# Cross-attention heads in three hi and lo passes instead of full fp32, with Strassen blocks moved between single chunks

## The chip, the cores and the metric

The kernel runs on one core of one Trainium2 chip. The metric is the device time of one execution in microseconds. The core has TensorE (PE; its weight loads are shown as PEld), VectorE (DVE), ScalarE (ACT), GpSimd (POOL) and SyncE (SP), which run side by side and wait for each other by semaphores. Transfers are issued from queues of SP, POOL and ACT.

## The reference

One decoder layer over 256 tokens of 1024 channels, all in float32. The part that the change touches is branch C, cross-attention of four heads of 128 channels into 256 memory tokens:

```python
def memory_cross_attention(q, mem_n, w_mem_kv):
    mk, mv = jnp.split(mem_n @ w_mem_kv, 2, axis=-1)
    # q, mk, mv are cut into XATTN_HEADS = 4 heads of 128
    lg = jnp.einsum('bshd,bmhd->bhsm', qh, kh).astype(jnp.float32) * (HEAD_DIM ** -0.5)
    p = jax.nn.softmax(lg, axis=-1).astype(q.dtype)
    return jnp.einsum('bhsm,bmhd->bshd', p, vh).reshape(B, S, C_WIDTH)

h = rms_norm(x, norm_g[layer])
(qa, ka, va, ga, ub, vb, gb, qc, gc, ma, mb, mc) = split_cols(h @ w_in[layer], IN_SPLITS)
out_c = memory_cross_attention(qc, rms_norm(mem, ...), w_mem_kv[layer]) * jax.nn.silu(gc)
y = sigmoid(ma) * (out_a @ w_branch_a) + sigmoid(mb) * (out_b @ w_branch_b) + sigmoid(mc) * (out_c @ w_branch_c)
return rms_norm(x + y @ w_out)
```

Branch A is causal attention with six heads of 128, branch B a gated product of tokens in chunks of 128.

## The kernel before, in words

**Chunks.** All weights pass TensorE in an order written out by `plan()`. A chunk is 128 x 1024 weights. For each chunk ScalarE makes a rounded high part (`split_hi`, L260, type fp32r) and VectorE the remainder (`split_lo`, L264); a product of two such numbers is then three fp32r passes, hi x hi, hi x lo and lo x hi (`mm3`, L448 to L450, and the same written out elsewhere). The kinds of chunk:

- "mvk" (8): memory values and keys; "tok" (4): part of the values of A and B; 
- "fea" (30): one head of q, k, qc, or 128 channels of a gate; `mm_fea`, L630, 8 passes of 512 columns and 8 of 256;
- "st" (70): the remaining input columns, by a Strassen scheme with seven products of half blocks; a block is two chunks of `mm_st`, L570, six passes of 512 columns each. Their weights are summed in two "form" buffers: loaded on SP (L233), added to by transfers on POOL (L236) or by VectorE (L240);
- "br" (16) and "out" (8): the branch and output projections, with `mm3`.

Chunks are split four ahead of their use, into five slots. Pairs of chunks that are not Strassen share one "raw" buffer; `load` (L214) fills it when the second chunk of the pair two before it is split.

**Planner.** Everything else is a list of units with an engine, an estimated duration, what it comes after, and a due chunk (class `Units`, L85 to L148). While the program is written out, `slot` puts a unit in ahead of or behind a chunk when its engine has room by the estimates, or when it is due. TensorE units must be ready by the estimate with 1.8 us to spare, or due. On the chip each engine then follows its own written order.

**Cross heads.** The queries are evicted by `join_half` (L633) to tile "cx"; the memory keys too, then multiplied by the memory's norm (`mkf`, L658); the values by `evict_mv` (L604, L608). Four chains for each head follow: `cs` with `c_scores` (L882, L886: two fp32 products of 256 columns), the maximum (L891) and the exponentials; `cn` normalizes; `cp` transposes (L781) and evicts the transposed weights (`c_pT_out`, L901); `cv` is `c_pv` (L903, L908: two fp32 products of 256 columns) and the eviction of the result (L914). Rope of branch A moves pairs of q and k by transfers on the SP queue (L769).

**Where order binds.** `cx` is one tile. Tiles of one tag share memory: a new tile waits for the last reader of the old one. "ga" and "gc" belong to the gates' chunks, "sg0" and "sg1" to the first gate's sums, "och" and "ocl" to the memory rows first and branch C's output later.

Of the kernel before, what the change touches and what calls it, by code (L numbers as in the profile page):

```python
# [24 lines left out]
F32 = mybir.dt.float32  # L25
# [3 lines left out]
OP = mybir.AluOpType  # L29
# [20 lines left out]


def plan():


    p = [("mvk", 0), ("vvb", 0)]
    st = [("st", (g, i)) for g in range(FAST) for i in ORDER]
    late = st[24:]
    del st[24:]
    for what in ("qc0", "", "qc2", "", "q0", "", "q1", "", "", "q2", "", "q3", "", "", "q4", "", "", "q5",
                 "", "", "ga0", "", "ga2", "", "", "ga4", "", "", "gc0", "", "", "gc2", "", "ub4", "", "", "gb4", "", ""):  # L60
        if not what:
            p.append(st.pop(0))
        elif what[0] == "q" and what[1] != "c":
            p += [("q", int(what[1])), ("k", int(what[1]))]
        else:
            p += [(what[:2], int(what[2]) + i) for i in range(2)]
    assert not st, len(st)
    br = [("br", ((h, a), (g, b))) for h, a, g, b in ((0, 0, 0, 1), (1, 0, 1, 1), (0, 2, 1, 2), (0, 3, 0, 4),
                                                      (0, 5, 1, 3), (1, 4, 1, 5), (0, 6, 0, 7), (1, 6, 1, 7))]
    for piece, n in zip(br, (2, 1, 2, 2, 2, 1, 1, 0)):  # L70
        p += [piece] + late[:n]
        del late[:n]
    return p
# [78 lines left out]
def tile_hybrid_layer(ctx: ExitStack, tc: tile.TileContext, mw, xT, mem, x, fin_g, ln_g, w, ws, w_sp, b_sp, b_spt, rope, out):  # L152
# [37 lines left out]
    for name, g in PLAN:  # L190
        if name == "mvk":
            chunks += [("mvk", HALVES[2 * i], HALVES[2 * i + 1]) for i in range(KD)]
        elif name in TOK:
            chunks += [("tok", name, g * 512, 2 * i) for i in range(4)]
        elif name in ("st", "br"):
            chunks += [("st", *g, i) if name == "st" else ("br", *g[i]) for i in range(2)]
# [7 lines left out]
    n_all = len(chunks)  # L204
    PLAIN = [j for j in range(n_all // 2) if chunks[2 * j][0] != "st"]

# [3 lines left out]
    def load_part(j, a, b):  # L210
        src = bass.AP(tensor=w.tensor, offset=w.offset + PLAIN.index(j) * 128 * PIECE + a, ap=[[PIECE, 128], [1, b - a]])
        nc.sync.dma_start(raw[j][:, a:b], src)

    def load(j):  # L214
        raw_alloc(j)
        parts = 2 if 18 <= j < 47 else 1
        for i in range(parts):
            load_part(j, i * PIECE // parts, (i + 1) * PIECE // parts)
# [31 lines left out]
    def split_alloc(c):  # L250
# [5 lines left out]
        hi[c], lo[c] = V["hi"][:, c % SPL, :], V["lo"][:, c % SPL, :]  # L256

    def split_hi(c, a=0, b=CH):
        o = (c % 2) * CH
        nc.scalar.activation(hi[c][:, a:b], raw[c // 2][:, o + a:o + b], AF.Copy)  # L260

    def split_lo(c, a=0, b=CH):
        o = (c % 2) * CH
        nc.vector.tensor_tensor(lo[c][:, a:b], raw[c // 2][:, o + a:o + b], hi[c][:, a:b].bitcast(F32),  # L264
                                OP.subtract)
# [353 lines left out]
    def mm_fea(c):  # L619
        _, name, h = chunks[c]  # L620
        src = V["n"]


        p = acc_bank()
        pa, pb = p[:, 0:S], p[:, S:2 * S]
        long = [(p, hi[c][:, hsl(k)], src[:, k].rearrange("p a s -> p (a s)")) for k in range(KD)]
        short = [(pa, lo[c][:, hsl(k)], src[:, k, 0, :]) for k in range(KD)]
        passes = short + long if c % 2 else long + short
        for i, (o, wt, m) in enumerate(passes):
            nc.tensor.matmul(o, wt, m, start=i == 0, stop=i == len(passes) - 1, skip_group_check=True)  # L630
        join_half(name, h, c, p)

    def join_half(name, h, c, p):  # L633
# [18 lines left out]
        elif name in ("qc", "mk"):  # L652
            i = int(name == "mk")
            cross_tile()
            join(V["cx"][:, i, h, :])
            if i and h % 2:
                u = V["cx"][:, 1, h - 1:h + 1, :]
                U.add(f"mkf{h}", DVE, 0.7, lambda: nc.vector.tensor_tensor(  # L658
                    u, u, bc["m"][:, None, :].to_broadcast([128, 2, S]), OP.mult),
                    after=[f"mk{h - 1}", f"mk{h}", "mrms"], first=True)  # L660
        elif name == "ub":
# [220 lines left out]
    def c_scores(h):  # L882
        cx = V["cx"]
        ST["cs", h] = ps = bank()
        for t in range(2):
            nc.tensor.matmul(ps[:, t * S:(t + 1) * S], cx[:, 0, h, tsl(t)], cx[:, 1, h, :], start=True, stop=True)  # L886

# [11 lines left out]
    def c_pT_out(h):  # L899
        ST["cT", h] = work.tile([128, 512], F32, name="pt", tag="pt", bufs=3)  # L900
        nc.scalar.activation(ST["cT", h], ST["cp", h], AF.Copy)  # L901

    def c_pv(h):  # L903
        p = ST["cT", h]
        mv = V["cx"][:, 2].rearrange("p (t a) b -> p t (a b)", t=2)
        ST["co", h] = ps = bank()
        for m in range(2):
            nc.tensor.matmul(ps[:, 0:S], mv[:, m, hsl(h)], p[:, m * S:(m + 1) * S], start=m == 0, stop=m == 1)  # L908

    def c_out(h):  # L910
# [3 lines left out]
        nc.scalar.activation(V["oc"][:, h, :], ST["co", h][:, 0:S], AF.Copy)  # L914

    for h in range(HC):
# [6 lines left out]
        U.chain(f"cp{h}", (PE, 0.44, lambda h=h: c_pT(h)), (ACT, 0.62, lambda h=h: c_pT_out(h)), after=[f"cn{h}"] + back("v", h))  # L923
        U.chain(f"cv{h}", (PE, 0.88, lambda h=h: c_pv(h)), (ACT, 0.4, lambda h=h: c_out(h)), after=[f"cp{h}", "mve"])

# [233 lines left out]
    for c in range(n_br + 4):  # L1159
# [14 lines left out]
        for e in {5: (), 6: (), 7: (9,), 8: (11,), 9: (12, 13)}.get(c, (s,) if s > 3 else ()):  # L1174
            if chunks[e][0] == "st":
                raw[e // 2] = form_tile(buf(*chunks[e][1:3]))
                came = ready[e]
            else:
                came = {4: 24.0, 5: 25.5}.get(e // 2, 0.0)
# [6 lines left out]
        s += c == 9  # L1186
        if s % 2 == 1 and s // 2 in PLAIN:
            q = PLAIN.index(s // 2) + 2
            if 4 < q < len(PLAIN):
                load(PLAIN[q])  # L1190
            if q == 6:
                load_mem()
# [132 lines left out]
```

## Time and profile before

| | |
|---|---|
| time, median of 3 runs | 316.98 us (316.41 to 317.22) |
| profiled execution | 316.41 us, span 314.7 us |
| TensorE | busy 307.0 us, 98% of the span |
| VectorE | 259.8 us, 83% |
| ScalarE | 228.2 us, 73% |
| GpSimd | 36.4 us, 12% |
| mean granted TensorE clock | 0.995 |

The span runs from the first to the last instruction. Busy time of TensorE counts overlapped passes once. A group's row has its line in the kernel, engine, operation, out<-in by the program's names, shapes, a count, and then busy us, mean ns of one, and idle time before it. A row of waits names who waited for whom, us in total, times, and the longest. A row of a timeline or of the chain has start and length in us.

### The profile page before, as it was taken

The page shows a single profiled execution, that of the slowest core. Times are in us where ns is not written, and L with a number is a line of the kernel's source. Part 1 is how long each engine was busy: PE and PEld are TensorE (multiplying, and loading weights), DVE is VectorE, ACT ScalarE, POOL GpSimd, SP SyncE. Part 2 cuts the span into 40 slices and gives each one's busy share as a digit, 9 for nine tenths or more (in the row PEclk, how much of TensorE's full clock was granted, in tenths as well). Part 3 has the DMA queues.
Part 4 walks back from the last instruction along what each step waited for, and adds up shares of the span by engine and source line. Part 5 has one row for each costly group of instructions (what it writes and reads, how often), then busy time and mean ns, then how long its engine had stood idle before and what let it go on. Part 6 is the DMA issues. An engine that isn't in the chain of part 4 may idle for free.

```text
span 314.7 us, 4438 instructions
## 1 busy us (share of the span) xinstructions
PE 307.0 (98%) x1542; PEld 259.1 (82%) x1542; DVE 259.8 (83%) x376; ACT 228.2 (73%) x357; POOL 36.4 (12%) x55
## 2 busy tenths in 40 slices
PE   7999999999999999999999999999999999999992
PEld 3888888888888888888888888888888887888982
DVE  2879998996689888877499799999896699989532
ACT  3876989556997668877996978778759565486333
POOL 1000040030011013005002102004010031000022
PEclk9999999999999999999999999999999999999997
DMA  7999999779659869958966999778999989943003
GB/s 194 408 390 421 403 351 234 305 209 202 190 187 237 293 214 223 209 204 187 323 202 175 192 336 292 166 246 189 219 347 274 313 212 194 394 147 133 2 5 129
DMA packets 20470, 75.14 MB, mean 239 GB/s; under 512 B 2656, under 2 KB 3680, under 8 KB 18016
## 3 DMA queue, kind: packets, MB, share of 16 engines
q1 hardware_dynamic: 15984, 59.00, 52.1%
q0 software_dynamic: 4320, 15.73, 27.6%
q8 instruction: 12, 0.20, 0.2%
q10 hardware_dynamic: 144, 0.13, 0.1%
q14 instruction: 10, 0.08, 0.1%
HBM read 73.02 MB, written 1.05 MB: 235 GB/s over the span
## 4 chain that ended last, share of the span: by engine, by line
PE 82%; DMA 7%; DVE 4%; issue 3%; ACT 2%; POOL 0%; ACTq 0%; SPq 0%; POOLq 0%; DVEq 0%
PE acc L630 27%; PE acc L570 18%; DMA form<-in_ws_dram 6%; PE aux L570 5%; PE acc L508 4%; PE acc L450 3%; PE acc L448 3%; PE acc L449 3%; PE aux L502 3%; DVE lo L264 2%; PE aux L781 2%; PE acc L481 2%; PE aux L481 2%; DMA raw<-in_w_dram 2%; PE aux L449 1%
## 5 line engine op out<-in xcount | busy, mean ns | idle before, releaser
L264 DVE TENSOR_TENSOR lo<-form,hi 128x1024 fp32r<-128x1024 f32 x70 | 84.8, 1221 | 15.4 <-ACT hi L260 14.8
L260 ACT ACTIVATE hi<-form 128x1024 fp32r<-128x1024 f32 x70 | 73.5, 1058 | 23.5 <-DMA form<-in_ws_dram 9.7
L264 DVE TENSOR_TENSOR lo<-raw,hi 128x1024 fp32r<-128x1024 f32 x58 | 70.1, 1222 | 10.2 <-ACT hi L260 10.0
L260 ACT ACTIVATE hi<-raw 128x1024 fp32r<-128x1024 f32 x58 | 60.9, 1057 | 9.0 <-DMA raw<-in_w_dram 2.7
L630 PE MATMUL acc<-n,hi 128*128 128x512 f32 x240 | 60.2, 393 | 0.0
L236 POOL DMA_DIRECT2D form<-in_ws_dram x30 | 26.1, 871 | 229.2 <-DVE lo L264 83.3
L630 PEld LDWEIGHTS acc<-n,hi 128*128 128x128 f32 x240 | 44.0, 188 | 8.5
L570 PE MATMUL acc<-hi,s 128*128 128x512 f32 x96 | 32.7, 398 | 0.0
L630 PE MATMUL acc<-n,lo 128*128 128x256 f32 x240 | 32.6, 285 | 0.0
L630 PEld LDWEIGHTS acc<-n,lo 128*128 128x128 f32 x240 | 31.3, 191 | 1.3
L570 PE MATMUL acc<-hi,n 128*128 128x512 f32 x72 | 24.8, 401 | 0.0
L570 PEld LDWEIGHTS acc<-hi,s 128*128 128x128 f32 x96 | 18.0, 188 | 3.7
L570 PE MATMUL aux<-hi,s 128*128 128x512 f32 x64 | 20.7, 389 | 0.0
L570 PE MATMUL acc<-lo,s 128*128 128x512 f32 x48 | 18.7, 389 | 0.0
L570 PE MATMUL aux<-hi,n 128*128 128x512 f32 x48 | 15.8, 391 | 0.0
L570 PEld LDWEIGHTS acc<-hi,n 128*128 128x128 f32 x72 | 13.5, 188 | 2.7
L570 PEld LDWEIGHTS aux<-hi,s 128*128 128x128 f32 x64 | 12.0, 188 | 2.5
L570 PE MATMUL acc<-lo,n 128*128 128x512 f32 x36 | 14.0, 390 | 0.0
L643 ACT ACTIVATE qk<-acc 128x256 f32<-128x256 f32 x12 | 4.7, 389 | 11.1 <-PE acc L630 11.0
L570 PE MATMUL aux<-lo,s 128*128 128x512 f32 x32 | 12.6, 393 | 0.1
L240 DVE TENSOR_TENSOR form<-form,form 128x1024 f32<-128x1024 f32 x10 | 12.2, 1220 | 0.0
L570 PEld LDWEIGHTS aux<-hi,n 128*128 128x128 f32 x48 | 9.0, 188 | 1.9
(233 smaller groups left out, 578.7 us busy)
## 6 DMA issues: line engine op xcount, KB each, us to landing
raw<-in_w_dram SPq DMA_DIRECT2D x18, 1024.0 KB, 8.4
form<-in_ws_dram SPq DMA_DIRECT2D x30, 512.0 KB, 6.0
form<-in_ws_dram POOLq DMA_DIRECT2D x30, 512.0 KB, 8.4
raw<-in_w_dram SPq DMA_DIRECT2D x22, 512.0 KB, 6.9
st<-in_mw_dram SPq DMA_DIRECT2D x7, 384.0 KB, 7.4
raw<-in_w_dram SPq DMA_DIRECT2D x8, 256.0 KB, 6.9
xk<-in_x_dram SPq DMA_DIRECT2D x2, 512.0 KB, 7.3
xt<-in_xT_dram SPq DMA_DIRECT2D x2, 512.0 KB, 8.4
```

Of the source, the lines that this page charges most:

```text
L236: nc.gpsimd.dma_start(form_half(i, h), block(g, b, h), accum_op=OP.add)
L240: nc.vector.tensor_tensor(form_half(i, h), form_half(i, h), form_half(1 - i, h), OP.add)
L260: nc.scalar.activation(hi[c][:, a:b], raw[c // 2][:, o + a:o + b], AF.Copy)
L264: nc.vector.tensor_tensor(lo[c][:, a:b], raw[c // 2][:, o + a:o + b], hi[c][:, a:b].bitcast(F32), OP.subtract)
L448: nc.tensor.matmul(p, s_hi, m_hi, start=first, stop=False)
L449: nc.tensor.matmul(p, s_hi, m_lo, start=False, stop=False)
L450: nc.tensor.matmul(p, s_lo, m_hi, start=False, stop=last)
L481: nc.tensor.matmul(acc[name, o][t], src[:, k0 + i, tsl(t)], wt[c][:, i * 512:(i + 1) * 512], start=c == 8 and i + j == 0, stop=c == 11 and ...
L502: nc.tensor.matmul(acc["mv", 0][t][:, a:b], src[:, k, tsl(t)], wt[:, a:b], start=k + n == 0, stop=k == KD - 1 and n == len(parts) - 1)
L508: nc.tensor.matmul(p, wt, m, start=k == 0 and j < HC, stop=k == KD - 1 and j >= HC)
L570: nc.tensor.matmul(p, x[:, k0 + k, tsl(t)], wt[c][:, a * 512:(a + 1) * 512], start=first and a + j == 0, stop=half == 1 and a + j == 3, sk ...
L630: nc.tensor.matmul(o, wt, m, start=i == 0, stop=i == len(passes) - 1, skip_group_check=True)
```

## The change

The cross heads' products go through `mm3`. For that the queries, the keys, the values and the transposed weights each get a high part (ScalarE) and a low part (VectorE), in tiles that lie in tags not in use at that time. `cp` and `cv` get due chunks, counted back from the first ga chunk. The order is written out chunk by chunk in a string, in which "." is one Strassen block; against the order before, one block now stands between q1 and k1 (before: behind k1), one between q2 and k2 (before: behind k2), one between ga0 and ga1 (before: behind ga1). The other chunks keep their order. Loads are numbered by pairs of plain chunks, with the same pairs and the same parts.

```diff
+SEQUENCE = ("qc0 qc1 . qc2 qc3 . q0 k0 . q1 . k1 . q2 . k2 q3 k3 . . q4 k4 . . q5 k5 . . ga0 . ga1 ga2 ga3 . . "
+            "ga4 ga5 . . gc0 gc1 . . gc2 gc3 . ub4 ub5 . . gb4 gb5 . . w00 w01 . . w10 w11 . w02 w12 . . w03 w04 "
+            ". . w05 w13 . . w14 w15 . w06 w07 . w16 w17")
...
-    for what in ("qc0", "", "qc2", "", "q0", "", "q1", "", "", "q2", "", "q3", "", "", "q4", "", "", "q5",
-                 "", "", "ga0", "", "ga2", "", "", "ga4", "", "", "gc0", "", "", "gc2", "", "ub4", "", "", "gb4", "", ""):
...
     def evict_mv():
-        cross_tile()
+        for n, tag in (("mvh", "gc"), ("mvl", "ga")):
+            slot_tile(n, [128, 2, CW], tag, F32R)
         for t in range(2):
-            h = V["cx"][:, 2, 2 * t:2 * t + 2, :].rearrange("p a b -> p (a b)")
-            nc.scalar.activation(h, acc["mv", 0][t], AF.Copy, scale=rstm[:, t:t + 1])
+            p, f = acc["mv", 0][t], rstm[:, t:t + 1]
+            h = V["mvh"][:, t, :]
+            nc.scalar.activation(h, p, AF.Copy, scale=f)
+            later(f"mvl{t}", DVE, 0.7, scaled_lo, V["mvl"][:, t, :], p, f, h, due=now[0] + 2)
...
+                def hi_part():
+                    if n + "h" not in V:
+                        slot_tile(n + "h", [128, HC, S], high, F32R)
+                        slot_tile(n + "l", [128, HC, S], low, F32R)
+                    nc.scalar.activation(V[n + "h"][:, hs, :], u, AF.Copy)
...
+                U.chain(f"{name}l{h}", (ACT, 0.62, hi_part),
+                        (DVE, 0.7, lambda: sub_lo(V[n + "l"][:, hs, :], u, V[n + "h"][:, hs, :])),
+                        after=[f"mkf{h}"] if i else [f"qc{h - 1}", f"qc{h}", "mrow"], first=True,
+                        due=10 ** 6 if i else c + 4)
...
         for t in range(2):
-            nc.tensor.matmul(ps[:, t * S:(t + 1) * S], cx[:, 0, h, tsl(t)], cx[:, 1, h, :], start=True, stop=True)
+            mm3(ps[:, t * S:(t + 1) * S], V["qch"][:, h, tsl(t)], V["qcl"][:, h, tsl(t)], V["mkh"][:, h, :],
+                V["mkl"][:, h, :], True, True)
...
-        ST["cT", h] = work.tile([128, 512], F32, name="pt", tag="pt", bufs=3)
+        ST["cT", h] = work.tile([128, 512], F32R, name="pt", tag="pt", bufs=3)
         nc.scalar.activation(ST["cT", h], ST["cp", h], AF.Copy)
 
+    def c_pT_lo(h):
+        if h < 2:
+            slot_tile(f"ptl{h}", [128, 512], ("ub", "v1")[h], F32R)
+        sub_lo(V[f"ptl{h % 2}"], ST["cp", h], ST["cT", h])
...
-            nc.tensor.matmul(ps[:, 0:S], mv[:, m, hsl(h)], p[:, m * S:(m + 1) * S], start=m == 0, stop=m == 1)
+            ms = slice(m * S, (m + 1) * S)
+            mm3(ps[:, 0:S], V["mvh"][:, m, hsl(h)], V["mvl"][:, m, hsl(h)], p[:, ms], low[:, ms], m == 0, m == 1)
...
-        U.chain(f"cs{h}", (PE, 0.88, lambda h=h: c_scores(h)), (DVE, 0.9, lambda h=h: c_max(h)),
+        U.chain(f"cs{h}", (PE, 0.72, lambda h=h: c_scores(h)), (DVE, 0.9, lambda h=h: c_max(h)),
...
-                after=[f"qc{h}", f"mkf{h | 1}", "sqrts"] + back("p", h))
+                after=[f"qcl{h | 1}", f"mkl{h | 1}", "sqrts"] + back("p", h))
...
+        U.chain(f"cp{h}", (PE, 0.44, lambda h=h: c_pT(h)), (ACT, 0.62, lambda h=h: c_pT_out(h)), after=[f"cn{h}"] + back("v", h), due=[G0 - 12 + h, G0 - 11 + h])
+        U.chain(f"cv{h}", (DVE, 0.68, lambda h=h: c_pT_lo(h)), (PE, 0.72, lambda h=h: c_pv(h)), (ACT, 0.4, lambda h=h: c_out(h)),
+                after=[f"cp{h}", "mvl0", "mvl1"], due=[G0 - 10 + h, G0 - 6 + h, G0 - 5 + h])
```

More of the change, by code (lines that the diff above doesn't have):

```diff
@@ L56, in plan @@
     st = [("st", (g, i)) for g in range(FAST) for i in ORDER]
-    late = st[24:]
-    del st[24:]
-    for what in ("qc0", "", "qc2", "", "q0", "", "q1", "", "", "q2", "", "q3", "", "", "q4", "", "", "q5",
-                 "", "", "ga0", "", "ga2", "", "", "ga4", "", "", "gc0", "", "", "gc2", "", "ub4", "", "", "gb4", "", ""):
-        if not what:
+    for what in SEQUENCE.split():
+        if what == ".":
             p.append(st.pop(0))
-        elif what[0] == "q" and what[1] != "c":
-            p += [("q", int(what[1])), ("k", int(what[1]))]
+        elif what[0] == "w":
+            p.append(("br", (int(what[1]), int(what[2]))))
         else:
-            p += [(what[:2], int(what[2]) + i) for i in range(2)]
+            p.append((what[:-1], int(what[-1])))
     assert not st, len(st)
[L68 to L72, printed above, removed]
     return p
@@ L194, in tile_hybrid_layer @@
             chunks += [("tok", name, g * 512, 2 * i) for i in range(4)]
-        elif name in ("st", "br"):
-            chunks += [("st", *g, i) if name == "st" else ("br", *g[i]) for i in range(2)]
+        elif name == "st":
+            chunks += [("st", *g, i) for i in range(2)]
+        elif name == "br":
+            chunks.append(("br", *g))
         else:
@@ L203, in tile_hybrid_layer @@
             chunks += [("out", c, kh * 4), ("out", c, kh * 4 + 2)]
-    n_all = len(chunks)
-    PLAIN = [j for j in range(n_all // 2) if chunks[2 * j][0] != "st"]
+    PLAIN = [c for c, k in enumerate(chunks) if k[0] != "st"]
+    place = {c: divmod(m, 2) for m, c in enumerate(PLAIN)}
     def raw_alloc(j):
@@ L215, in load @@
         raw_alloc(j)
[L216 removed]
+        parts = 2 if 12 <= j < 22 else 1
         for i in range(parts):
@@ L627, in mm_fea @@
         short = [(pa, lo[c][:, hsl(k)], src[:, k, 0, :]) for k in range(KD)]
-        passes = short + long if c % 2 else long + short
+        passes = short + long if place[c][1] else long + short
         for i, (o, wt, m) in enumerate(passes):
@@ L1186, in tile_hybrid_layer @@
         s += c == 9
[L1187 to L1190, printed above, removed]
+        if place.get(s, (0, 0))[1]:
+            q = place[s][0] + 2
+            if 4 < q < len(PLAIN) // 2:
+                load(q)
             if q == 6:
@@ L1254, in tok @@
         return m.reshape(2, 4, 128, 512).transpose(0, 2, 1, 3).reshape(-1)
-    def fea(ms):
-        r = np.stack([m.reshape(KD, 128, 128) for m in ms]).transpose(2, 0, 1, 3)
-        return r.reshape(-1)
     wkv = np.asarray(w_mem_kv)[0]
@@ L1272 @@
     for name, g in PLAN:
-        if name == "st":
-            continue
-        if name == "br":
-            parts.append(np.stack([br[i] for i in g], axis=1).reshape(-1))
+        if name in ("st", "br"):
+            if name == "br":
+                two.append(br[g].reshape(128, -1))
         elif name == "mvk":
@@ L1281 @@
         else:
-            two.append(cols[name][:, g * 128:(g + 1) * 128])
-            if len(two) == 2:
-                parts.append(fea(two))
-                two = []
+            two.append(cols[name][:, g * 128:(g + 1) * 128].reshape(KD, 128, 128).transpose(1, 0, 2).reshape(128, -1))
+        if len(two) == 2:
+            parts.append(np.stack(two, axis=1).reshape(-1))
+            two = []
     w = np.concatenate(parts + [wo.reshape(-1)])
```

35 lines of the change are left out of this document (19 added, 16 removed).

## The prediction

> **What bounds the kernel now.** I read the page first, then TensorE's waits, then the chain of work that ended last in order of time, then timelines of single stretches.
>
> ```profile
> span 314.7 us, 4438 instructions
> PE 307.0 (98%) x1542; PEld 259.1 (82%) x1542; DVE 259.8 (83%) x376; ACT 228.2 (73%) x357; POOL 36.4 (12%) x55
> ...
> PEclk9999999999999999999999999999999999999997
> ```
>
> TensorE is busy for 98% of the span at the full granted clock. Its own waits, in the whole run:
>
> ```profile
> PE aux L354 <- PEq L1314: 0.8, 1, 0.8
> PE acc L508 <- ACT hi L422: 0.8, 1, 0.8
> ```
>
> Both lie in the first 8 us. Between them and the output's last products TensorE is never seen idle, so the span is the sum of what TensorE streams, plus head and tail. Whatever takes TensorE time away shortens the span by that much, as long as the engines that feed it keep up.
>
> The cross heads' products stand in that chain. Columns are start, length in us, and the work; "x" counts records, two for each fp32 product of 256 columns:
>
> ```profile
> 67.27 2.59 PE aux L886 x12
> ...
> 94.18 1.73 PE aux L908 x8
> 95.91 0.86 PE aux L886 x4
> ...
> 101.37 0.86 PE aux L908 x4
> ...
> 112.41 0.86 PE aux L908 x4
> ```
>
> That is 2.59 + 1.73 + 0.86 + 0.86 + 0.86 = 6.90 us for 32 records, 0.216 us each, 0.43 us for a product.
>
> **The products.** Four heads have two score products and two value products each, 16 in all. Each becomes three fp32r passes of 256 columns: 48 passes. The timeline of TensorE shows passes of that form, each with its own weight load, in the fea chunks and (the same helper of three passes) at the end:
>
> ```profile
> 79.75 2.08 PE L630 MATMUL acc<-n,lo 128*128 128x256 f32 x16
> 81.66 2.00 PE L630 MATMUL acc<-n,hi 128*128 128x512 f32 x8
> ...
> 293.14 0.28 PE L448 MATMUL aux<-hi,y 128*128 128x256 f32 x1
> ...
> 293.85 0.40 PE L1105 MATMUL aux<-xks,identr 128*128 128x256 f32 x2
> ```
>
> From 79.75 to 81.66 there are 16 passes: 0.119 us each. From 293.14 to 293.85 there are 6: 0.118. I take 0.120, rounded up. New cost 48 x 0.12 = 5.76 us; saved 6.90 - 5.76 = **1.14 us**. The bounds are narrow: 0.118 gives 1.24, 0.125 would give 0.90.
>
> The Trainium skill, "FP8 and Floating Point Precision", section "TensorE Precision Notes", says that true FP32 takes four passes through the array. By that rule alone three passes leave 3/4 of 6.90, a saving of 1.73 us and a median of 315.25. The rows say less, because a reduced-precision pass of 256 columns takes 0.12 us and a quarter of an fp32 product only 0.108; the rows decide.
>
> **What is added on VectorE and ScalarE.** Prices by groups of like instructions (count, busy us, mean ns):
>
> ```profile
> L993 DVE TENSOR_TENSOR obl<-aux,obh 128x512 fp32r<-128x512 f32 x2 | 1.4, 684 | 0.0
> L970 DVE SCALAR_TENSOR_TENSOR ut<-aux,b_col,ut 128x256 f32<-128x256 f32 x4 | 1.7, 476 | 0.0
> L877 DVE SCALAR_TENSOR_TENSOR vb<-vb,lst,lng 128x768 f32<-128x768 f32 x2 | 2.0, 1012 | 0.0
> L729 ACT ACTIVATE n<-xt 128x512 fp32r<-128x512 f32 x4 | 2.5, 625 | 0.0
> ```
>
> - Splits of the queries and of the memory keys, two pairs each: ScalarE 4 x 0.63 = 2.5 us, VectorE 4 x 0.68 = 2.7 us.
> - Low part of the memory values: two scalar_tensor_tensor of 512 columns, halfway between 476 and 1012 ns, 0.74 each: 1.5 us. The high part replaces an eviction of the same size.
> - Low part of the transposed weights, one per head: 4 x 0.68 = 2.7 us on VectorE.
>
> VectorE gets 6.9 us and ScalarE 2.5 us more. None of it is on the path if it fits into their slack. Where it falls:
>
> ```profile
> 39.40:64.50 25.10, 25.10 (x135) 21.74 (x135) 24.18 (x33) 19.50 (x29) 3.59 (x8) 1.00 0.87 282
> 64.50:92.80 28.30, 28.30 (x154) 24.64 (x153) 21.39 (x30) 22.21 (x40) 3.45 (x4) 1.00 0.80 203
> 92.80:116.00 23.20, 23.20 (x118) 19.75 (x117) 21.42 (x40) 15.98 (x27) 1.81 (x3) 1.00 0.85 246
> ```
>
> Columns: stretch, its length, then busy time of PE, PEld, DVE, ACT, POOL. In the first stretch VectorE has 0.9 us free, and there come 2.9 us that are due by the planner (two query splits, two value parts) and, where it sees room, 1.4 us for the keys. So for a while VectorE runs late. What covers that is the distance between a chunk's split and its first use:
>
> ```profile
> 48.45 2.36 DVE L264 TENSOR_TENSOR lo<-form,hi 128x1024 fp32r<-128x1024 f32 x2 [0.77 <-ACT hi L260]
> ...
> 73.11 0.42 DVE L645 TENSOR_TENSOR qk<-qk,acc 128x256 f32<-128x256 f32 x1 [2.69 <-ACT qk L643]
> ...
> 86.02 1.21 DVE L264 TENSOR_TENSOR lo<-raw,hi 128x1024 fp32r<-128x1024 f32 x1
> ```
> ```profile
> 54.92 0.39 PE L570 MATMUL acc<-lo,n 128*128 128x512 f32 x1
> ...
> 89.78 1.20 PE L630 MATMUL acc<-n,lo 128*128 128x256 f32 x8
> ```
>
> The second split of the row at 48.45 ends at 50.81 and is first used at 54.92: 4.1 us of cover against 2.2 to 2.9 us put in before it. At 73.11 VectorE stood idle for 2.69 us, and the stretch from 64.5 to 92.8 has 6.9 us free, so it catches up there. The least cover of that part is at 86.02: done at 87.23, used at 89.78, 2.55 us, behind the exponentials on ScalarE. Cost taken: 0. If the cover at 50.81 is overrun by all 4.3 us, 0.2 us is lost there. In the third stretch 1.8 us are free for 2.7 us; the rest is late by 0.9 us.
>
> **The order.** One Strassen block (two chunks) moves in between q1 and k1, one between q2 and k2, one between ga0 and ga1. No chunk is added; TensorE streams the same. Each block takes its ScalarE and VectorE splits with it, and its refill on the SP or POOL queue. On the SP queue the rope transfers of the first pair wait for k1, now later by the two Strassen chunks ahead of it, 2.7 us (twelve passes of 512 columns; a row of the chain has them):
>
> ```profile
> 44.95 2.72 PE acc L570 x12
> ```
> ```profile
> 63.70 10.37 SPq L769 DMA_DIRECT2D mid<-qk  x4
> 79.98 1.47 SPq L233 DMA_DIRECT2D form<-in_ws_dram  x2
> ```
>
> The transfers hold SP until 74.07; the next issue behind them is at 79.98, so 2.7 us later still leaves 3.2 us. The weight loads are issued at the split of a pair's second chunk, as before; k1's and k2's are two chunks later, ahead of and behind those transfers as before. Cost 0; without that cover the refill at 79.98 would be late by what is missing. That fewer Strassen splits stand in a row gives VectorE back cover, which I count as nothing.
>
> **The late stage.** The least cover of the run lies here, rows of VectorE, TensorE and the chain:
>
> ```profile
> 260.21 1.22 DVE L264 TENSOR_TENSOR lo<-form,hi 128x1024 fp32r<-128x1024 f32 x1
> ```
> ```profile
> 261.49 0.50 PE L570 MATMUL aux<-lo,s 128*128 128x512 f32 x1
> ```
> ```profile
> 216.10 0.24 PE acc L450
> ...
> 224.15 6.56 DMA form<-in_ws_dram
> ...
> 235.83 10.84 DMA form<-in_ws_dram
> ...
> 246.78 1.07 ACT hi L260
> ```
>
> The split ends at 261.43 and TensorE starts at 261.49: it had waited some 0.3 us. The chain back goes through VectorE, ScalarE and two transfers to a TensorE product at 216.10. As this stage begins at TensorE, and its order of chunks is unchanged, it moves forward with TensorE by 1.14 us and keeps its 0.3 us. I take 0 to 0.6 us as the bounds of that wait, from none to double, since the two transfers above, of one size, took 6.56 and 10.84.
>
> **Sum.** Profiled execution: span 314.7, time 316.41, so 1.7 us lie around it. New span 314.7 - 1.14 = 313.56, time 315.27. The median of the runs shown is 316.98, 0.57 above the profiled one; on its footing **315.84**, -0.36%. A measurement of this kernel tells some 0.3% (0.95 us) from no change, so the forecast stands just outside.
>
> **Rivals.**
>
> A. *The late chain does not move.* If what starts the transfers from 216 on is VectorE's backlog rather than TensorE, the 1.14 us come back as a wait at 261: span 314.7, median 316.98. For it: cover of 0.06 us there. Against it: the chain's own start at 216.10. With lesser waits of 0.3 to 0.9 us anywhere: 316.1 to 316.7. Together 0.27.
>
> B. *Slower: value products wait for VectorE.* Before, they waited only for ScalarE's eviction of the transposed weights; now one VectorE subtraction comes between, on a queue that is 92% busy from 92.8 to 116, and TensorE waits in order with the whole chunk stream behind it.
>
> ```profile
> 90.69 1.11 ACT L901 ACTIVATE pt<-aux 128x512 f32<-128x512 f32 x2
> ...
> 98.69 0.59 ACT L901 ACTIVATE pt<-aux 128x512 f32<-128x512 f32 x1
> ```
> ```profile
> 94.02 1.89 PE L908 MATMUL aux<-pt,cx 128*128 128x256 f32 x8
> ...
> 101.21 1.02 PE L908 MATMUL aux<-pt,cx 128*128 128x256 f32 x4
> ```
>
> The eviction ended at 99.28 and the product began at 101.21, 1.9 us later: this is about the margin of 1.8 us that the planner keeps. The subtraction takes 0.68, and the planner moves the product back by its own estimate of it; TensorE waits only if VectorE is later than planned by more than 1.8 us. Two whole splits ahead of it (2 x 1.22) plus late data could make 0.8 us for each head, 3.2 in all: 315.84 + 3.2 = 319.0. It decides "slower" from 0.52 us a head (2.1 us in all). Chance 0.14, other losses of that size in it.
>
> C. *Weight loads come to the front.* 48 passes need 48 loads against 32.
>
> ```profile
> L630 PEld LDWEIGHTS acc<-n,lo 128*128 128x128 f32 x240 | 31.3, 191 | 1.3
> ```
>
> If none of a load's 0.19 us were hidden, a pass would take 0.12 + 0.19 = 0.31, 48 of them 14.9 us: median 316.98 + 8.0 = 325. But these very loads stand in stretches of 0.119 us a pass, so they overlap. Chance 0.01. The Trainium skill, "TensorE: Matmul & The Clock Gate", section "Part 3: Packing small matmuls — row/col tiling", states that weight loads overlap running matmuls only where row groups differ; all rows here use all 128, and the trace does not agree.
>
> **Chances and range.** The forecast has 0.58, A 0.27, B 0.14, C 0.01. The forecast's own range is 315.3 to 316.3: 0.118 a pass and no wait at 261, or a wait of 0.5. The median's own scatter (0.26% between the runs' ends) puts some of it inside 0.3%: of the forecast's 0.58, 0.50 is faster by more than 0.3% and 0.08 within; A adds 0.27 within; B and C are slower: 0.50, 0.35, 0.15. The range for eight in ten goes from 315.1 to 317.5, which takes in all of A and leaves out most of B.
>
> **What would show it.** Right: the new score and value passes 0.12 us each, in groups of 0.72 us a head; TensorE without waits from 40 to 200; the rows of the late stage 1.1 us earlier, with the same short wait near 260. Wrong: TensorE waiting for VectorE's new low part or for a split between 45 and 66 (B, or the cover too small); a wait before the product at 261 grown by 1.1 us (A); passes at 0.3 us (C).

## The result

The changed kernel takes 319.63 us (median of 8 runs, 318.92 to 321.58); the kernel before, run beside it on the same chip, 317.10 us. The ratio is 1.0086 (95% interval 1.0057 to 1.0116): slower by some 2.5 us, where 1.14 us less was forecast. It lies outside the range given. The profiled execution took 319.2 us with a span of 317.5, 2.8 us more than before.

Medians differ a little from chip to chip, so each kernel below has its ratio to the kernel before, run beside it. One execution of held35, the profiled one, was disturbed (a span of 629 us); neither its time nor its profile is used.

The page of the changed kernel:

```profile
span 317.5 us, 4485 instructions
PE 308.3 (97%) x1558; PEld 259.4 (82%) x1558; DVE 264.6 (83%) x386; ACT 229.0 (72%) x361; POOL 37.5 (12%) x55
...
PEclk9999999999999999999999999999999999999997
```

VectorE is busy 4.8 us more; its ten new instructions sum to the 6.9 us that the prediction took (1.4 for each of the queries', keys' and values' low parts, 2.7 for the transposed weights'), but consecutive instructions overlap in the records. TensorE is busy 1.3 us more, although its new passes are shorter: passes that are held up count as busy. TensorE's waits (line, what it waited for, us in total, times, longest):

```profile
PE aux L801 <- ACT p L833: 0.7, 1, 0.7
PE acc L573 <- ACT va L580: 0.7, 1, 0.7
PE aux L801 <- ACT mid L939: 0.6, 1, 0.6
PE aux L573 <- DVE lo L267: 0.4, 1, 0.4
```

Before, there was no such row after the first 8 us; the 0.3 us near 261 that the prediction worked out is not listed as a wait. None of the four names a new operation: the transposes wait for ScalarE (L801), a Strassen chunk waits for an eviction (L580), one for its split (L267). These are the waits that the profile itself shows as idle. From one product's start to the next, the waits near 79, 109 and 122 cost 0.9, 0.8 and 1.2 us more than the same products undisturbed, and the value products near 126 a further 0.3.

By 213 us nearly the whole loss is there. The same product, the first pass of the first chunk of branch a's projection, in the two chains of waits, before and after:

```profile
210.89 0.23 PE acc L448
```
```profile
213.41 0.23 PE acc L451
...
263.07 1.23 DVE lo L267
264.34 1.43 PE aux L573 x5
```

2.52 us late at 213, and 264.34 - 261.49 = 2.85 at the wait of the late stage. Since the shorter products give 1.14 us back, 2.52 + 1.14 = 3.7 us were lost by 213; the places above make up 3.2 of them, and the rest lies in small pieces that are not placed here.

**The passes cost what was forecast.** TensorE's timeline, the scores of three heads:

```profile
80.80 0.28 PE L451 MATMUL aux<-mkh,qch 128*128 128x256 f32 x1
...
82.83 0.28 PE L453 MATMUL aux<-mkh,qcl 128*128 128x256 f32 x1
82.95 0.40 PE L573 MATMUL acc<-hi,s 128*128 128x512 f32 x1
```

18 passes from 80.80 to 82.95: 0.119 us each, 0.72 a head; their weight loads of 0.19 us each do not show. But before, the scores went in at 67.27. They are 13.5 us later.

**Why so late.** VectorE's timeline:

```profile
73.68 1.23 DVE L267 TENSOR_TENSOR lo<-form,hi 128x1024 fp32r<-128x1024 f32 x1
...
75.14 0.69 DVE L459 TENSOR_TENSOR mkl<-cx,mkh 128x512 fp32r<-128x512 f32 x1
77.86 1.23 DVE L267 TENSOR_TENSOR lo<-form,hi 128x1024 fp32r<-128x1024 f32 x1 [2.02 <-ACT hi L264]
79.00 0.69 DVE L459 TENSOR_TENSOR mkl<-cx,mkh 128x512 fp32r<-128x512 f32 x1
```

The keys' low parts have no due chunk. The planner holds them back until it sees room on VectorE, at chunks 28 and 29, and the scores wait for both. So the softmax, the transposes and the value products of all cross heads come later too, among rope and branch A.

**Where it is lost.** First, near 79 us: GpSimd's, ScalarE's and TensorE's timelines.

```profile
66.83 0.86 POOL L234 DMA_DIRECT2D form<-in_ws_dram  x1 [22.12 <-DVE qk L651]
67.36 0.74 POOL L705 MEMSET mask<- 128x64 f32 x4
68.09 3.36 POOL L708 TENSOR_SCALAR_AFFINE_SELECT mask<-mask 128x64 f32<-128x64 f32 x2
71.40 2.63 POOL L234 DMA_DIRECT2D form<-in_ws_dram  x3
```
```profile
76.76 1.06 ACT L264 ACTIVATE hi<-form 128x1024 fp32r<-128x1024 f32 x1 [3.13 <-DMA form<-in_ws_dram]
77.73 1.04 ACT L264 ACTIVATE hi<-raw 128x1024 fp32r<-128x1024 f32 x1
78.68 0.58 ACT L580 ACTIVATE va<-acc 128x512 f32<-128x512 f32 x1
```
```profile
79.31 0.50 PE L573 MATMUL acc<-hi,s 128*128 128x512 f32 x1 [0.67 <-ACT va L580]
```

GpSimd works in order: the mask's set-up (4.1 us) sits between two form additions, three of them start late, ScalarE stands 3.13 us for the block's data with the eviction of `va` queued behind, and TensorE waits for the eviction. Second, near 109 us; SP, VectorE, GpSimd, ScalarE and TensorE in turn:

```profile
79.48 2.48 SPq L789 DMA_DIRECT2D mid<-qk  x4
```
```profile
89.00 0.01 DVE L794 LOAD_MASK_SELECT mid<-mid  x1 [2.58 <-DMA mid<-qk]
```
```profile
95.50 0.86 POOL L234 DMA_DIRECT2D form<-in_ws_dram  x1 [21.46 <-DVE lo L267]
```
```profile
107.94 1.06 ACT L264 ACTIVATE hi<-form 128x1024 fp32r<-128x1024 f32 x1 [3.35 <-DMA form<-in_ws_dram]
```
```profile
109.59 0.66 PE L801 MATMUL aux<-ident,p 128*128 128x128 f32 x4 [0.62 <-ACT mid L939]
```

Where the softmax used to be, the planner now sees VectorE free and puts the rope work of the first pair there, at 89.00 (before: 99.84). The transfers aren't in yet. VectorE stands 2.58 us, the splits behind it release the next form addition at 95.50 (before: 93.08), the transfer lands later, ScalarE waits 3.35, and `mid` comes too late for the transposes. Third, near 122 us: the fourth head's transposes. Their chunk had passed, so the planner put them in with no margin, and ScalarE still scales the weights:

```profile
121.46 1.59 ACT L833 ACTIVATE p<-p,rc 128x256 f32<-128x256 f32 x4
```
```profile
122.01 0.95 PE L801 MATMUL aux<-ident,p 128*128 128x128 f32 x4 [0.71 <-ACT p L833]
```

So each loss is a short stall on an in-order queue, handed on over two or three engines. Which decision is behind them is the question of the runs.

### The profile page after: what moved, and what is told of

Its sections match the earlier page's. It is cut to its first block, busy times and chain, and to the rows that moved or that the text cites. A ratio compares the mean times of both kernels' runs of the same rounds, so it can differ in the third digit from the quotient of the medians.

```text
span 317.5 us, 4485 instructions
## 1 busy us (share of the span) xinstructions
PE 308.3 (97%) x1558; PEld 259.4 (82%) x1558; DVE 264.6 (83%) x386; ACT 229.0 (72%) x361; POOL 37.5 (12%) x55
## 4 chain that ended last, share of the span: by engine, by line
PE 66%; DMA 11%; DVE 8%; issue 8%; ACT 4%; POOL 1%; ACTq 0%; POOLq 0%
PE acc L636 18%; DMA form<-in_ws_dram 11%; PE acc L573 11%; PE aux L573 6%; DVE lo L267 5%; PE aux L505 4%; PE acc L511 4%; PE acc L452 3%; PE acc L453 3%; PE acc L451 3%; ACT hi L264 2%; PE acc L484 2%; PE aux L484 2%; PE aux L801 1%; PE aux L452 1%
## 5 line engine op out<-in xcount | busy, mean ns | idle before, releaser
L267 DVE TENSOR_TENSOR lo<-form,hi 128x1024 fp32r<-128x1024 f32 x70 | 84.6, 1221 | 15.2 <-ACT hi L264 15.2
L267 DVE TENSOR_TENSOR lo<-raw,hi 128x1024 fp32r<-128x1024 f32 x58 | 70.0, 1222 | 8.4 <-ACT hi L264 8.1
L573 PEld LDWEIGHTS acc<-hi,n 128*128 128x128 f32 x72 | 13.5, 188 | 2.9 <-issue 0.2
L573 PEld LDWEIGHTS acc<-lo,s 128*128 128x128 f32 x48 | 9.1, 189 | 1.5
```

The costliest lines, as they stand in the source:

```text
L267: nc.vector.tensor_tensor(lo[c][:, a:b], source(c)[:, a:b], hi[c][:, a:b].bitcast(F32), OP.subtract)
L573: nc.tensor.matmul(p, x[:, k0 + k, tsl(t)], wt[c][:, a * 512:(a + 1) * 512], start=first and a + j == 0, stop=half == 1 and a + j == 3, sk ...
```

## The experiments

Two theories at first. T1: the added VectorE work makes the scores late, and the late chain costs. T2: the new order of chunks does it. Line numbers in the diffs are left out; they are against the changed kernel.

**One part alone.** new_order_fp32 puts the products back to fp32 and takes all splits out, but keeps the order; old_order keeps the passes and puts the order back; values_only and scores_only keep one half of the passes with its splits, in the new order. Where the value products are fp32, their due chunks are gone too.

```diff
-SEQUENCE = ("... q0 k0 . q1 . k1 . q2 . k2 q3 k3 . . ... ga0 . ga1 ga2 ga3 . . "
+SEQUENCE = ("... q0 k0 . q1 k1 . . q2 k2 . q3 k3 . . ... ga0 ga1 . ga2 ga3 . . "    # old_order
...
-            mm3(ps[:, t * S:(t + 1) * S], V["qch"][:, h, tsl(t)], V["qcl"][:, h, tsl(t)], V["mkh"][:, h, :],
-                V["mkl"][:, h, :], True, True)
+            nc.tensor.matmul(ps[:, t * S:(t + 1) * S], V["cx"][:, 0, h, tsl(t)], V["cx"][:, 1, h, :], start=True, stop=True)    # values_only
...
-            mm3(ps[:, 0:S], V["mvh"][:, m, hsl(h)], V["mvl"][:, m, hsl(h)], p[:, ms], low[:, ms], m == 0, m == 1)
+            nc.tensor.matmul(ps[:, 0:S], V["mvh"][:, m, hsl(h)], p[:, ms], start=m == 0, stop=m == 1)    # scores_only
```

> The new order of chunks with the cross heads' products left in full fp32, as before. T1 (the added work on VectorE makes the key splits late, the scores go in 14 us later and the whole cross chain with them): scores stand at 67 us as before, no wait of TensorE over 0.3 us between 40 and 200, time within 0.6 us of before. T2 (the order: Strassen blocks brought forward make the refill of the form buffers late): the waits of 0.8 us near 78 and 108 are there, time 1.5 to 2.5 us above before.

> Three passes for the cross heads, chunks in the order of before. T1: scores stay late (after 80 us), TensorE loses 2 to 4 us in waits, time 1 to 4 us above before. T2: no waits, the saving of 1.1 us shows, time 1.1 us under before.

> New order; only the products with the values in three passes, scores in fp32, so queries and keys are not split (2.5 us less on ScalarE, 2.7 us less on VectorE). T1: scores at 67 to 69 us, half of the saving (0.57 us) shows, waits under 0.4 us: time 0 to 0.6 us under before. T2: as slow as the new order alone, 1 to 2.5 us above before.

> New order; only the scores in three passes, products with the values in fp32 and without due chunks (no low part of values or of transposed weights, 4.2 us less on VectorE). T1: key splits still late, scores after 78 us, TensorE waits 1 us or more, time 0.5 to 3 us above before; without the due chunks the waits of 1.2 us before the transposes near 121 are gone. T2: as slow as the new order alone.

Measured: new_order_fp32 317.67 us, 1.0014 (0.9979 to 1.0049); old_order 328.61, 1.0365 (1.0286 to 1.0444); values_only 317.62, 1.0005 (0.9973 to 1.0038); scores_only 321.51, 1.0130 (1.0066 to 1.0195). T2 falls: the order alone is free, and with the passes in it is worth some 9 us. Those 9 us are not traced to one decision: old_order has twelve waits of 0.15 to 1.1 us between 106 and 273 us. Taken alone, the value part costs nothing, and the score part more than both together, so the parts do not add up. Nor does the saving of up to 0.6 us show that T1 expected of the value part: values_only waits 0.9 us near 208 and 1.2 near 263.

**Late scores or added work.** held adds no work to new_order_fp32 but makes the scores wait for chunk 30; unused takes scores_only, makes all splits of queries and keys, and lets the scores read the unsplit tiles.

```diff
-                after=[f"qcl{h | 1}", f"mkl{h | 1}", "sqrts"] + back("p", h))
+                after=[f"qc{h}", f"mkf{h | 1}", "sqrts", "c30"] + back("p", h))    # held; unused without "c30"
```

> The new order of chunks with all cross heads' products in fp32 as before, and nothing added on VectorE or ScalarE; only the scores are held back until chunk 30 is through, so that they start at chunk 31 or 32, as late as with three passes. The order alone measured 1.0014 of the kernel before. Theory L (what costs is that the scores come 14 us late, so that the softmax of the cross heads, their transposes and value products fall among branch A's heads): 319 to 321 us, TensorE waits of 0.3 to 1 us between 100 and 135 us. Theory W (what costs is the added VectorE and ScalarE work itself, by making splits late where it stands): within 0.3% of the order alone, 316.7 to 318, no new TensorE wait.

> As the run with three-pass scores only (1.013 of the kernel before), but the scores stay in fp32 and read the joined queries and keys; the four high parts on ScalarE (2.5 us) and the four low parts on VectorE (2.7 us) are still made, and nobody waits for them. Left out of use, not of the work. The scores can start at chunk 25. Theory L (lateness of the scores costs): 317 to 318 us, scores near 70 us, no wait of more than 0.3 us between 100 and 135. Theory W (the added work itself costs): 320 to 322 as the scores-only run, with waits for splits near 61 to 80 us.

Measured: held 320.67 us, 1.0105 (1.0055 to 1.0156); unused 317.90, 1.0017 (0.9986 to 1.0047). In time that is L on both counts: the four subtractions and four copies are hidden when nobody waits for them, and late scores cost 3 us with no added work at all. In place it is not. held's waits:

```profile
PE aux L573 <- DVE lo L267: 1.9, 2, 1.1
PE aux L573 <- ACT hi L264: 1.5, 1, 1.5
...
PE aux L573 <- DVE ut L978: 0.5, 1, 0.5
```

All of them lie after 206 us. Nothing was lost between 100 and 135, where L expected it.

**How late.** held28 and held35 are held with chunk 28 and 35.

> As the held run (new order, all products in fp32, nothing added on VectorE or ScalarE, scores held back until chunk 30: 1.0105 of the kernel before), but the scores are held until chunk 28: they go in around chunk 30 instead of 24 (free) or 32 (held). Theory L, lateness by itself: the loss grows with the hold, so about three quarters of the held run's loss, 319 to 320.3 us. Theory R, the planner lays out everything behind the late scores anew and what is lost is a matter of which transfers then meet in the late stage from 200 us on: no order with the hold, anything from 317 to 321; between 316.5 and 318 speaks for R.

> The same with the scores held until chunk 35, so that they go in at chunk 37, 13 chunks (some 27 us) late. Theory L: more than the held run's loss, 321 to 324 us, as the heads' softmax, transposes and value products fall together with branch A's. Theory R: no order with the hold, 317 to 321, and the waits, if any, after 200 us.

> The kernel of held35 once more (scores in fp32, held until chunk 35: 1.0163 of the kernel before), for its profile alone. By the held run, where nothing was lost before 200 us and 4 us behind it, the waits should again lie at 206, 250 and 264 us, longer than there: some 6 us in sum. If lateness costs where the heads' work piles up, there are waits between 110 and 140 us.

Measured: held28 317.92 us, 1.0029 (1.0009 to 1.0050); held35 322.49 (median of three), 1.0163 (1.0127 to 1.0199); held35b, one execution, 323.22. With the scores put in at chunk 24 (new_order_fp32), 30, 32 and 37 the ratio is 1.0014, 1.0029, 1.0105 and 1.0163: it grows, but not in step with the hold. Six chunks are nearly free, the next two cost over 2 us. The changed kernel has them at chunk 31, at that edge. Between 32 and 37 the clock has a part: the execution of held35 with a mean granted clock of 0.998 took 320.61 us, as held, and the two with 0.984 and 0.985 took 323.02 and 322.49. So held28 speaks for R, and held35 in time for L; but held35b's waits again lie in the late stage, near 249 to 256, as R has it.

**The low parts out of the way.** pool gives the four low parts of queries and keys to GpSimd; keysdue makes the keys' parts due at chunk 23; nolow leaves out the low parts and lets the passes read the high ones in their place; lowfree is nolow with the low parts made for nobody.

```diff
-                        (DVE, 0.7, lambda: sub_lo(V[n + "l"][:, hs, :], u, V[n + "h"][:, hs, :])),
+                        (POOL, 1.3, lambda: nc.gpsimd.tensor_tensor(V[n + "l"][:, hs, :], u,
+                                                                    V[n + "h"][:, hs, :].bitcast(F32), OP.subtract)),    # pool
...
-                        due=10 ** 6 if i else c + 4)
+                        due=23 if i else c + 4)    # keysdue
...
-            mm3(ps[:, t * S:(t + 1) * S], V["qch"][:, h, tsl(t)], V["qcl"][:, h, tsl(t)], V["mkh"][:, h, :],
-                V["mkl"][:, h, :], True, True)
+            mm3(ps[:, t * S:(t + 1) * S], V["qch"][:, h, tsl(t)], V["qch"][:, h, tsl(t)], V["mkh"][:, h, :],
+                V["mkh"][:, h, :], True, True)    # nolow, lowfree
```

> The changed kernel with one edit: the four low parts of queries and keys (VectorE 4 x 0.68 us) go to GpSimd, which is busy 12% of the span. The key splits no longer stand in VectorE's queue, the scores start at chunk 26. If the late key splits cause the loss: the waits near 78, 108 and 121 us go, TensorE keeps the 1.14 us, and the time is 315.8 to 317.0. If the loss comes from the value part or the order, 319 to 320 as the changed kernel. If the subtraction is slow on GpSimd (over 3 us each) its form additions come late and new waits for splits appear: above 319.

> The changed kernel with one number changed: the keys' high and low parts are due at chunk 23 instead of when there is room, so that they are queued ahead of later chunks' splits and the scores go in at chunk 27 instead of 31. Same instructions as the changed kernel. If the loss is the late scores meeting the added VectorE work: the waits near 78, 108 and 121 to 126 us shrink and the time is 316.5 to 318.5. If VectorE has no room for the key splits between 40 and 70 us at all: TensorE waits for splits between 55 and 75 us by 1 to 3 us, and the time is 319.5 to 322.

> The changed kernel with all 48 passes and all high parts, but without the four low parts of queries and keys: the score passes read the high parts in their place (the low parts' terms of the scores are so left out). VectorE has 2.7 us less, the scores no longer wait for it and go in at chunk 26 instead of 31. If the low parts (their time or their place in VectorE's queue) are what costs: the waits near 78, 108 and 121 to 126 us go and the time is 315.5 to 317.3, the saving of 1.14 us less what the late stage takes. If something else in the three-pass scores costs (the passes, the high parts on ScalarE): 319 to 320.

> As nolow, but VectorE still makes the four low parts, and nobody waits for them: same work on every engine as the changed kernel. If it is the scores' wait for the low parts (lateness) that costs: within 0.3% of nolow, 315.5 to 318. If the 2.7 us of VectorE work by itself cost: 319 to 320.5 as the changed kernel, with waits of TensorE for splits near 70 to 80 us.

Measured: pool 324.96 us, 1.0226 (1.0178 to 1.0274); keysdue 320.58, 1.0090 (1.0059 to 1.0121); nolow 329.59, 1.0344 (1.0297 to 1.0391); lowfree 324.75, 1.0184 (1.0127 to 1.0241). Four ways to have the scores early, and none as fast as the kernel before. In pool it is GpSimd's queue; GpSimd's timeline and TensorE's:

```profile
73.64 0.85 POOL L234 DMA_DIRECT2D form<-in_ws_dram  x1 [0.60 <-DVE lo L267]
74.20 2.81 POOL L678 TENSOR_TENSOR mkl<-cx,mkh 128x512 fp32r<-128x512 f32 x2
```
```profile
75.83 0.58 PE L452 MATMUL aux<-mkl,qch 128*128 128x256 f32 x1 [4.19 <-POOL mkl L678]
```

A subtraction takes 1.4 to 1.5 us there against 0.69, and stands behind form additions that wait for VectorE. The Trainium skill, "GPSIMD Engine Reference", section "4.1 Engine selection", has it that GpSimd is about twice as slow in two-input operations and advises VectorE; the first agrees (1.41 against 0.69), and the larger loss here is the queue, 4.19 us; in this execution the clock adds to it, granted at 0.50 from 73.7 to 80.6 us. In keysdue the added work costs where it stands: TensorE waits 1.07 us for a split until 71.42, as its expectation has it for a VectorE without room.

nolow has 2.7 us less work than the changed kernel and is some 8 us slower by the ratios. Its waits and two rows of SP:

```profile
PE aux L837 <- DMA qk<-mid: 2.4, 2, 1.4
PE aux L990 <- DVE sigs L587: 1.8, 1, 1.8
```
```profile
140.36 2.06 SPq L231 DMA_DIRECT2D form<-in_ws_dram  x2
142.47 5.88 SPq L788 DMA_DIRECT2D qk<-mid  x8
```

The rope transfers of two pairs are issued together behind a refill that SP waited on, and branch A's scores wait for them. No low part is near. lowfree has the same waits at 145 and 215. So "late low parts" isn't the whole cause either. What the runs have in common is that the planner, given other units, places everything behind them anew; that this is what costs is argued from them, not shown by one.

**The early wait alone.** consts_early puts the mask's set-up ahead of the waiting form addition.

```diff
-    U.add("consts", POOL, 1.3, setup_consts, after=["sx0"], wait=6.0)
+    U.add("consts", POOL, 1.3, setup_consts, after=["mrms.0"], wait=6.0)
```

> The changed kernel with one edit: GpSimd's mask set-up, which in the changed kernel stood from 67.4 to 71.5 us behind a form addition that waited, is put in earlier, after the memory's norm. If this is what makes the waits of 0.83 and 0.11 us at 78.4 to 79.3 us, they go and the time falls by 0.9 us, to about 318.7. If the form is late without it (VectorE late behind the key splits), they stay and the time is within 0.3% of the changed kernel, 319.6.

Measured: 320.40 us, 1.0101 (1.0049 to 1.0153). TensorE's wait, ScalarE's timeline and a stretch (columns as in the prediction, the third from the right is the granted clock):

```profile
PE aux L801 <- ACT mid L939: 2.1, 1, 2.1
```
```profile
109.14 1.06 ACT L264 ACTIVATE hi<-form 128x1024 fp32r<-128x1024 f32 x1 [3.19 <-DMA form<-in_ws_dram]
```
```profile
112.00:114.00 2.00, 2.00 (x6) 1.62 (x5) 1.93 (x7) 1.45 (x3) 0.00 (x0) 0.50 0.96 363
```

The wait at 79 is gone, and the one at 122 with it. But the one at 109 grew from 0.6 to 2.1 us, its block's data reaching ScalarE at 109.14 instead of 107.94, and in this execution the clock behind it was halved. Taking a stall away moved the next one, and the time can't be told from the changed kernel's.

The set-up alone does not make the wait at 79. In held, whose scores come as late, it stands at the same place, but the form addition ahead of it starts at 64.29 instead of 66.83, and TensorE doesn't wait there. The 2.5 us between are the added work: from 50.68 to 66.20 the changed kernel's VectorE goes on without a wait, and its rows hold the two low parts of the values and the two of the queries more.

**The layout fixed.** frozen has the changed kernel's instructions but no planner: every unit goes in at the step where held28 had it, from a written list; the added ones at the places that their expectation names.

```diff
-        u = next((u for u in self.todo if self.fits(u, i, pe, now)), None)
+        u = next((u for u in self.todo if u[0] == wanted[0]), None)    # wanted: this step's names from the list
```

> The changed kernel, instruction for instruction (48 passes, all high and low parts), but the planner's choice is replaced by a written list: every unit at the step at which the held28 kernel (fp32 products, scores at chunk 30, 1.0029 of the kernel before) had it; the added units stand where the changed kernel had them (value low parts at 16, query splits at 17 and 21, keys' high parts at 25), the keys' low parts at 26 and 28, the low parts of the transposed weights directly behind their eviction. Theory P (the loss is the planner's new layout, the added work itself is hidden): held28 less the 1.14 us of the passes, ratio 0.996 to 1.001, 316.0 to 317.4 on the scale of 317.0 for the kernel before, no wait of over 0.3 us between 10 and 200 us. Theory W (the added 6.9 us of VectorE work costs wherever it stands): 1.006 to 1.012, with waits for splits or low parts between 45 and 125 us.

> frozen, with the one edit in the late stage that made old_values_gate faster than the kernel before (0.9928): branch b's additions of gated sums as units at chunks 114, 115 and 120 instead of ahead of the split that TensorE waits for near 261 us. Theory P: the wait near 261 us goes, 0.990 to 0.996 (313.9 to 315.8). Theory W: 1.003 to 1.009. If a transfer sets the wait near 250 us as in the held runs, that part stays: up to 0.4 us more.

Measured: frozen 323.18 us, 1.0144 (1.0111 to 1.0176); frozen_gate 322.17, 1.0110 (1.0076 to 1.0144). Both expectations of P fail, and at one place. VectorE, TensorE and the stretches behind, of frozen:

```profile
90.94 1.23 DVE L291 TENSOR_TENSOR lo<-form,hi 128x1024 fp32r<-128x1024 f32 x1 [3.16 <-ACT hi L288]
...
95.61 1.28 DVE L483 TENSOR_TENSOR ptl<-aux,pt 128x512 fp32r<-128x512 f32 x2
```
```profile
105.96 0.39 PE L476 MATMUL aux<-ptl,mvh 128*128 128x256 f32 x1 [2.64 <-DVE ptl L483]
```
```profile
107.00:108.50 1.50, 1.50 (x6) 1.23 (x5) 1.50 (x5) 1.20 (x2) 0.00 (x0) 0.63 0.58 210
108.50:110.00 1.50, 1.50 (x6) 1.22 (x6) 1.43 (x5) 0.00 (x0) 0.00 (x0) 0.50 1.03 320
110.00:112.00 2.00, 2.00 (x16) 2.00 (x16) 1.36 (x2) 0.79 (x3) 0.00 (x0) 0.80 0.74 252
```

TensorE waits 4.3 us in all for the low parts of the transposed weights, 1.70 until 96.35 and 2.64 until 105.96, and in this execution the lower clock takes 1.5 x 0.37 + 1.5 x 0.50 + 2.0 x 0.20 = 1.7 us more. Three splits of 1.22 us, late because VectorE stood 3.16 us for ScalarE, are ahead of the first; ahead of the second stand the layer norm's statistics, a maximum, a split and the rope work. One chunk lay between the eviction and the product, as for the first two heads of the changed kernel, which loses only a few tenths of a us there: its low parts start as soon as the eviction ends, those of frozen 1.3 and 4.1 us later. W, by which the added work costs wherever it stands, had expected waits for low parts: they came, and the time is above its range too.

Up to 92 us frozen has no new wait: 18 of the 48 passes and all splits of queries, keys and values were free in this layout. Its form addition is as late as the changed kernel's (66.87) and `va` is evicted at 78.95, but the scores stand from 78.51 to 80.67, where the changed kernel's TensorE waited. So the wait at 79 takes three things together: the set-up's place, the added work ahead of it, and scores that are not there yet.

Without the two waits and the clock the profiled execution, 323.63 us, would have taken 317.6, on a chip where the kernel before takes 318.32. Two executions with a mean granted clock of 0.999, in which the clock can't have taken 1.7 us, took 322.11 and 322.95: 317.8 and 318.6 without two such waits. That is worked out, not shown, and whether any of the saving is left in it stays open: no run had this layout with later value products. In frozen_gate the wait of 1.2 us near 268 is gone, but 0.4 and 0.8 us came up near 257.

**The late stage.** old_values is values_only in the old order; old_values_gate then makes two additions of branch b into units.

```diff
-                if br != "a":
+                if br == "b":
+                    later(f"yb{c}{t}", DVE, 0.7, lambda y, sg: nc.vector.tensor_tensor(y, y, sg, OP.add), y, sg, due=c + 3)
+                elif br != "a":
                     nc.vector.tensor_tensor(y, y, sg, OP.add)
```

> Three passes for the value products alone, scores in fp32 as before, and the old order of chunks: with the new order the same measured 1.0005 of the kernel before, saving 0.6 us up to 200 us and losing it at 207 and 261.6 us. If the new order helps only where the scores are split (three passes for all lost 9 us more in the old order): the same as with the new order, 316.4 to 318.2. If the new order helps by itself: 319 or more. It is also the smallest change of the set, and could come out ahead of the kernel before by the 0.6 us that its passes save, 316.5.

> Three passes for the value products alone in the old order (0.9992 of the kernel before), and one edit in the late stage: branch b's two additions of gated sums (VectorE, 2 x 0.69 us at 258.4 and 259.8 us) are no longer put directly at the chunk's end, ahead of the split that TensorE waits 1.04 us for at 260.6, but as units that the planner places within three chunks. If VectorE's queue sets that wait: it falls by 1.0 us, and the time to 315.4 (315.0 to 316.2). If a transfer sets it: no change, 316.4.

Measured: old_values 316.42 us, 0.9992 (0.9969 to 1.0016); old_values_gate 316.05, 0.9928 (0.9898 to 0.9958), on a chip where the kernel before took 318.6. VectorE and TensorE of old_values, then all of old_values_gate's waits:

```profile
259.76 0.69 DVE L1095 TENSOR_TENSOR sig<-sig,sigs 128x512 f32<-128x512 f32 x1
260.37 1.22 DVE L267 TENSOR_TENSOR lo<-form,hi 128x1024 fp32r<-128x1024 f32 x1
```
```profile
261.65 0.50 PE L573 MATMUL aux<-lo,s 128*128 128x512 f32 x1 [1.04 <-DVE lo L267]
```
```profile
PE aux L357 <- PEq L1324: 0.8, 1, 0.8
PE acc L511 <- ACT hi L425: 0.7, 1, 0.7
PE aux L790 <- DVE sigs L587: 0.4, 1, 0.4
```

The wait of 1.04 us is gone; 0.4 comes up near 208. This version beats the kernel before in the direct comparison, and the changed one by its median. How much is the edit's can't be said closely: old_values ran on another chip, and between the two medians there is 0.37 us, less than the 1.0 expected.

## Why the prediction was wrong

**The products: right.** 0.119 us a pass, 48 of them some 5.7 us in place of 6.90. The rule of four passes for fp32 would have given 1.73; the rows were the better guide. Weight loads stayed hidden (C).

**"Cost taken: 0" for the added VectorE and ScalarE work: the step that failed.** The busy-time sums weren't what was wrong: 6.9 us came, and the part for queries and keys was hidden while nobody waited for it (unused, 1.0017). What the step left out are dependences: it looked at the cover of the chunks' splits, 4.1 us and 2.55, and not at what waits for the new units or behind them. Key low parts without a due chunk go in when the planner sees room; the scores wait for them and come 13.5 us later, and all units behind are placed anew. The low parts of values and queries delay the form addition behind them on VectorE's queue by 2.5 us. The two covers it watched were enough: no wait for a split appeared there. Some 3.7 us were lost, most of it at places that it didn't look at: near 79, 109 and 122.

**The order, "cost 0": right alone, wrong together.** new_order_fp32 is 1.0014, but for three passes the new order is a help of some 9 us. The rope transfers moved 15.8 us (63.70 to 79.48), not 2.7, since the planner places them; with the order alone that stays hidden.

**The late stage: right for the change, bounds too narrow.** It moved with TensorE and kept a wait of 0.4 us, within 0 to 0.6. In values_only, held and old_values the same wait is 1.0 to 1.2, and in the two with three-pass value products it took back what these save.

**Rivals.** A isn't what happened: the loss was there by 213 us. B gave 319.0 and so came nearest in time, by another way: value products waiting for their low parts make up 0.3 of the 3.7 us. Its mechanism is real, though: 4.3 us in frozen.

**What stays open.** Of the three early waits only the one at 79 is shown, by held, consts_early and frozen, which each lack one of its three conditions; those at 109 and 122 are read from the rows. For the one at 109 speaks held, whose rope work came as early, at 87.46, but whose transfers, issued at 77.12, were in: no wait. Against it speaks scores_only, whose VectorE stood 2.57 us for them at 87.74 and whose TensorE did not wait there. That the loss as a whole comes of where units are put, not of an operation's price, rests on unused, nolow, lowfree and the clean first 92 us of frozen; keysdue and frozen's later waits show that the added work has no free place everywhere. Nor were the waits in the late stage traced to one decision each. That some layout keeps the 1.14 us with all 48 passes is not shown: none of those tried did.

## What to carry over

Where a planner places work by room, price an added unit by what waits for it, by what it delays on its queue and by when the planner will put it in, not by its own time alone; then ask what fills the room that its late consumers leave. A kernel with one engine at 98% has no slack to absorb the stalls that a new layout makes, so a saving of 0.4% is smaller than the scatter between layouts of nearly the same instructions (0.993 to 1.037 here). Take such savings one at a time, smallest change first, and look at the thinnest cover in the run before spending work elsewhere.

## What was not expected of the hardware

A wait of TensorE can cost more than its length. After single waits of 2.06 us (consts_early) and 2.64 us (frozen) the granted clock fell to 0.50 for some 3.4 us, about a us after TensorE had started again, and took a further 1.7 us in frozen; after two waits of 1.5 and 0.8 us close together in held it stayed at 1.00, as after all of the changed kernel's. But in held35b, after two waits of the same 1.5 and 0.8 us, it fell and stayed at 0.50 for 6.8 us. So the length of the waits does not settle it, and not every execution of a kernel has the fall: frozen's mean clock lay between 0.990 and 0.999. The Trainium skill, "TensorE: Matmul & The Clock Gate", section "Part 1: The HAM clock gate (the "warmup" mystery)", tells of half rate after an idle window of about 3.4 us; here less than that was enough in these executions.
